# Seven small experts of a mixture-of-experts step in 64-row slots, two column tiles of plain fp32 at once

## The chip, the cores and the metric

The kernel runs on one core of one Trainium2 chip. The metric is the device time of one execution in microseconds (us): 1438.26 us, the median of 3 runs (1433.28 to 1438.53).

## What is computed

The reference is one inference step of a two-layer decoder for 512 prompt tokens and 8 samples, 520 tokens in all, of 1,024 features. Each layer has a mixer (layer 0: convolution and differential attention; layer 1: mLSTM), a layer norm, a mixture of experts, a second layer norm and a gated embedding. The part that matters here is the mixture of experts: a token chooses one of four groups and two of the group's four experts, so there are 1,040 pairs of token and expert in each layer.

```python
def hier_moe(x, w_group, w_router, w_gate, w_up, w_down):
    ...
    y = jnp.zeros_like(xt)
    for e in range(N_EXPERTS):                      # 16 experts
        hid = jax.nn.silu(xt @ w_gate[e]) * (xt @ w_up[e])   # 1024 x 512, twice
        y = y + gate[:, e:e + 1] * (hid @ w_down[e])         # 512 x 1024
    return y.reshape(b, t, d)
```

All of it is in float32. An expert's weights are 6.29 MB, so each layer reads 100.7 MB of them.

## The kernel before

`route` (L1010) works out, on VectorE, the group and the two experts of each token and each token's rank within its experts (`rank`, from 1; 0: no member). `moe` (L1049) then goes through the experts 0 to 15 in their own order, a block of 128 slots each.

For a block, `indices` (L1070) makes a one-hot matrix of ranks against slots, and from it, with small matmuls, the rows' numbers; empty slots get a number past the end. `gather` (L1086) fetches the rows by an indirect DMA on POOL. `tokens` (L1164) transposes them (8 blocks of 128) and takes each element apart into two fp32r parts, high and low. `parts` (L1175) loads a weight matrix in two loads of 1 MB and takes it apart likewise, 1,024 columns at a time: ScalarE casts (L129), VectorE subtracts (L130). `product` (L1184) and `mm3` (L133) multiply: high by high, high by low, low by high (L134 to L136), each 128 x 128 by 128 x 512. `hidden` (L1191) is silu(gate) times up, `hidden_T` (L1197) its transpose in parts, `down` (L1206) the third product, scaled by the slot's gate on ScalarE (L1223) and added to the rows of `ya` in DRAM by an indirect DMA on POOL (L1224). An expert has 24 matmuls for each of its three matrices, 72 in all. The down products of an expert come behind the next one's gate and up (only expert 13's come earlier).

Loads go through `load_w` (L138) into rings of 1 MB buffers (`wbuf`, L150): 14 buffers at first (`moe_pools`, L762), and from expert 10 on (`ESW`, L1290) the 5 buffers of two pools, as the others are wanted for what follows. Eight loads (gate and up of experts 0 and 1) are issued while the mixer ends (`moe_load`, L771). The ring's loads 8 to 13 are issued on POOL's queue, the others on SP's, in the order in which the experts need them; each waits until the buffer's last reader is done.

Behind `rank`, `moe` prepares blocks 0 and 1, then works out the gates (L1115 to L1144, `vals` as three bfloat16 parts) and, from the experts' counts, how many further blocks of 128 rows are needed (L1146 to L1159, `nbi`). Every engine reads that number (L1160) before it goes on; the further blocks (`overflow`, L1227) come behind the last expert, with weights by a register, and none are needed here. `ple_load` (L1342) queues the weights of the gated embedding behind the last expert's.

Of the kernel before, what the change touches and what calls it, by code (L numbers as in the profile page):

```python
# [8 lines left out]
F32 = mybir.dt.float32  # L9
# [3 lines left out]
I32 = mybir.dt.int32  # L13
# [9 lines left out]
T = TP + NS  # L23
# [7 lines left out]
MAXOV = (2 * T) // (CAP + 1)  # L31
# [22 lines left out]
              ("bm", 8), ("p16", 1), ("nhalf", 5), ("slots", 128), ("strict", 128), ("ids", 10), ("eidx", 16)]  # L54
# [8 lines left out]
def shape_constants():  # L63
# [29 lines left out]
    c["eidx"] = np.broadcast_to(np.arange(16, dtype=np.float32), (128, 16))  # L93
    big = np.zeros((128, CW), np.float32)
# [18 lines left out]
class K:  # L113
# [24 lines left out]
    def load_w(self, src):  # L138
        """a weight view of 8 KB per partition, into the next of the weight buffers"""
        w = self.wbuf()  # L140
        self.w_now = self.split_pools or not NW2 + NW3 < self.wturn <= GQ
# [39 lines left out]
    # work behind a product, one stage after each of the next products  # L181
# [3 lines left out]
    def behind(self, gen):  # L185
        """each stage behind what is traced by then: the weights' loads and parts and the products"""
# [17 lines left out]
    def split_w(self, w, l, h=None):  # L204
        """parts of w [128, a, c]: the low one in l [128, a * c], the high one in h or a tile of its own"""
# [5 lines left out]
    def hbuf(self):  # L211
        """a tile for a high part"""
# [4 lines left out]
    def lbuf(self):  # L217
        """a tile for two low parts, from the ring of the first weight buffers"""
# [117 lines left out]
    def to_T(self, x, n, m, xh, xl):  # L336
        """x [n tokens, 1024] -> columns of x^T, split"""
# [9 lines left out]
    def even(self):  # L347
# [4 lines left out]
        # mz: what the last rows need longest, where only parts of weights follow  # L352
        with tc.tile_pool(name="mz", bufs=1) as mz, tc.tile_pool(name="mx", bufs=1) as mx, tc.tile_pool(name="mx2", bufs=2) as mx2:
# [73 lines left out]
            # decode: rows of the cache (half page groups of 4 tokens)  # L427
# [68 lines left out]
            def attn(hp, i):  # L496
# [34 lines left out]
                # enough for the first token tile  # L531
# [3 lines left out]
            def norm_o(o, n, nh, hp, cols):  # L535
                """o [n, nh, 128]: rms norm over the last axis, scale, transpose into oT"""
# [14 lines left out]
            # convolution branch  # L551
# [41 lines left out]
            def dec_softmax():  # L593
                # decode softmax over 1024 cached keys and the new one
# [36 lines left out]
                # weight of the new token, [b, hp]  # L631
# [44 lines left out]
            # small loads, behind those of the weights  # L676
# [36 lines left out]
            def decode_tail():  # L713
                """what the samples' attention has left, and their tokens' norm"""
# [11 lines left out]
            # output projection by token tiles  # L726
# [28 lines left out]
    def mixer_pools(self):  # L755
        """what a mixer needs up to its output projection lies at the far end, where the experts' weights follow"""
# [14 lines left out]
    def moe_load(self, i, a, b):  # L771
        """the first weights of the experts, a up to b"""
# [5 lines left out]
    def norm_consts(self, p):  # L778
        """gains and offsets of the norms by feature, for both layers"""
# [13 lines left out]
    def router_consts(self):  # L793
        """router weights with the norm's gain folded in, the part of its offset, their sums negated, for both layers"""
# [21 lines left out]
    def mix_load(self, i):  # L816
        """the weights of the output projection, in rows"""
# [5 lines left out]
    def mix_split(self, own):  # L823
        """their parts: the high ones over x^T; own(k): a tile for the parts k and k + 1, where rows lie over x^T"""
# [146 lines left out]
        # router logits, of the rows before the norm, then with its mean and deviation  # L971
# [14 lines left out]
        # x1 for the experts, alpha * x1 to add their outputs to  # L986
# [13 lines left out]
    def rstd(self, tile, st, n):  # L1000
        """mean in column 0 and 1 / sqrt(var + eps) in column 3, from bn_stats"""
# [8 lines left out]
    def route(self):  # L1010
        """groups and experts of the tokens, the members of each expert and their ranks within it"""
# [7 lines left out]
        def places(l, n):  # L1019
            """how many are ahead: larger, or equal and before"""  # L1020
# [14 lines left out]
        # ranks from 1 (0: no member)  # L1035
# [13 lines left out]
    def moe(self, i):  # L1049
# [5 lines left out]
        with tc.tile_pool(name="exp", bufs=2) as p2:  # L1055
# [14 lines left out]
            def indices(rk):  # L1070
# [870 lines left out]
```

## Time and profile before

| | |
|---|---|
| median of 3 runs | 1438.26 us (1433.28 to 1438.53) |
| profiled execution | span 1429.4 us from the first to the last instruction; its own whole time is not told |
| PE (TensorE) | 1345.2 us busy, 94% of the span |
| DVE (VectorE) | 1062.8 us, 74% |
| ACT (ScalarE) | 811.3 us, 57% |
| POOL (GpSimd) | 256.8 us, 18% |
| DMA | 338.79 MB, mean 237 GB/s |
| expert stages | 345 to 661 us and 1031 to 1346 us |

How to read it: times are us from the span's start. PE's matmuls overlap one another in their pipeline, so that the work of one is seen from the start of one to the start of the next, not from its duration. The slices cut the span into 40 equal parts of 35.7 us. A window's row has for PE, PEld (weight loads of TensorE), DVE, ACT and POOL the busy us and the number of instructions, then the granted share of TensorE's clock (1.00 is 2.4 GHz, 0.50 is 1.2 GHz), the share of time in which the 16 DMA engines are busy, and GB/s. SPq is SP's sequencer, which issues DMAs; the length of such a row is the time until the issue was taken. A row of the timeline has start, length, engine, line, operation, what it writes and reads, and how many instructions were merged in it.

### The profile page before, as it was taken

Reading aid. Unit: us, or ns where it says so; the run is one execution under the profiler, and the core shown is the slowest. Engines: PE = TensorE matmul, PEld = TensorE weight load, DVE = VectorE, ACT = ScalarE, POOL = GpSimd, SP = SyncE. Lnnn points to the kernel's source line nnn. Section 1 sums busy time; section 2 is a strip of 40 time slices with the busy share of each in tenths; the row PEclk is TensorE's granted clock in tenths of the full one; section 3 lists DMA queues with packets and bytes.
Section 4 is the critical chain, followed back from the end, with each engine's and each line's share of the span. In section 5 each row is a group of like instructions: output and inputs, shape, how many; then the busy total and the mean of one; then the engine's idle time right before and its main releaser. Section 6 shows DMA issues by size and latency. Waiting matters only on the chain. (4 is left out here: it accounts for less than half of the span.)

```text
span 1429.4 us, 22095 instructions
## 1 busy us (share of the span) xinstructions
PE 1345.2 (94%) x8336; PEld 1121.1 (78%) x8336; DVE 1062.8 (74%) x1680; ACT 811.3 (57%) x1235; POOL 256.8 (18%) x262
## 2 busy tenths in 40 slices
PE   8999999995999999998989999999599999989997
PEld 7998877563888887777979988878388888867786
DVE  4679986457999998886745445775799999878672
ACT  3214554223888886777654332333378888777762
POOL 1013212324211112101130000101411111210113
PEclk9989999996999999999999999999799999999999
DMA  8458545876899969998342213483599997899821
GB/s 285 141 186 284 202 144 223 295 290 220 292 380 360 352 209 312 333 334 283 95 153 71 81 62 122 149 320 130 196 322 350 346 356 255 271 353 319 289 80 38
DMA packets 154254, 338.79 MB, mean 237 GB/s; under 512 B 17773, under 2 KB 56137, under 8 KB 150046
## 3 DMA queue, kind: packets, MB, share of 16 engines
q1 hardware_dynamic: 129438, 250.30, 49.6%
q0 software_dynamic: 24560, 86.96, 18.9%
q8 instruction: 67, 1.10, 0.3%
q14 instruction: 45, 0.37, 0.1%
q10 hardware_dynamic: 144, 0.07, 0.0%
HBM read 317.33 MB, written 36.48 MB: 248 GB/s over the span
## 5 line engine op out<-in xcount | busy, mean ns | idle before, releaser
L130 DVE TENSOR_TENSOR w<-w,sh 128x1024 fp32r<-128x1024 f32 x368 | 439.2, 1221 | 121.3 <-ACT sh L129 102.2
L129 ACT CAST sh<-w 128x1024 fp32r<-128x1024 f32 x368 | 376.0, 1050 | 247.8 <-PE acc L226 109.5
L135 PE MATMUL acc<-w,gh 128*128 128x512 f32 x512 | 204.1, 399 | 4.7 <-DVE w L130 4.4
L134 PE MATMUL acc<-sh,gh 128*128 128x512 f32 x512 | 207.2, 405 | 0.7 <-ACT sh L129 0.7
L136 PE MATMUL acc<-sh,gl 128*128 128x512 f32 x512 | 203.1, 397 | 0.8 <-DVE gl L130 0.8
L1224 POOL DMA_INDIRECT ya<-y,ix x32 | 52.2, 1631 | 386.0 <-ACT y L1223 375.9
L135 PEld LDWEIGHTS acc<-w,gh 128*128 128x128 f32 x512 | 97.3, 190 | 28.8 <-DVE w L130 8.4
L136 PEld LDWEIGHTS acc<-sh,gl 128*128 128x128 f32 x512 | 97.1, 190 | 23.9 <-DVE gl L130 1.7
L134 PEld LDWEIGHTS acc<-sh,gh 128*128 128x128 f32 x512 | 97.3, 190 | 22.8 <-ACT sh L129 1.9
L136 PE MATMUL acc<-sh,hl 128*128 128x512 f32 x256 | 102.7, 401 | 0.0
L134 PE MATMUL acc<-sh,hh 128*128 128x512 f32 x256 | 101.0, 395 | 0.9 <-ACT hh L129 0.9
L135 PE MATMUL acc<-w,hh 128*128 128x512 f32 x256 | 100.7, 394 | 0.0
L226 PE MATMUL acc<-x2h,w 128*128 128x256 f32 (+1 forms) x384 | 87.7, 291 | 0.9 <-ACT x2h L1463 0.4
L226 PE MATMUL acc<-xh,sh 128*128 128x256 f32 (+1 forms) x384 | 85.4, 301 | 2.0 <-ACT sh L129 1.2
L226 PE MATMUL acc<-xh,w 128*128 128x256 f32 (+1 forms) x384 | 81.1, 292 | 0.0
L226 PE MATMUL acc<-x3h,sh 128*128 128x256 f32 (+1 forms) x384 | 81.0, 291 | 0.0
L226 PE MATMUL acc<-xl,sh 128*128 128x256 f32 (+1 forms) x384 | 81.0, 292 | 0.0
L130 DVE TENSOR_TENSOR w<-wpair,sh 128x1024 fp32r<-128x1024 f32 x64 | 76.1, 1220 | 3.8 <-PE acc L135 2.0
L226 PE MATMUL acc<-x3l,sh 128*128 128x256 f32 (+1 forms) x384 | 78.5, 284 | 0.0
L226 PE MATMUL acc<-x3h,w 128*128 128x256 f32 (+1 forms) x384 | 78.1, 283 | 0.0
L129 ACT CAST sh<-wpair 128x1024 fp32r<-128x1024 f32 x64 | 65.6, 1051 | 14.4 <-PE acc L136 14.4
L258 PE MATMUL tps<-cst,w 128*128 128x128 f32 (+1 forms) x352 | 54.6, 287 | 13.5 <-DMA w<-xd,ix 9.3
(512 smaller groups left out, 2869.6 us busy)
## 6 DMA issues: line engine op xcount, KB each, us to landing
w<-in_w_exp_gate SPq DMA_DIRECT2D x52, 1024.0 KB
w<-in_w_exp_up SPq DMA_DIRECT2D x46, 1024.0 KB
w<-in_w_exp_down SPq DMA_DIRECT2D x46, 1024.0 KB
w<-in_w_in_even SPq DMA_DIRECT2D x12, 1024.0 KB
w<-in_w_in_odd SPq DMA_DIRECT2D x12, 1024.0 KB
wpair<-in_w_exp_up SPq DMA_DIRECT2D x10, 1024.0 KB
wpair<-in_w_exp_down SPq DMA_DIRECT2D x10, 1024.0 KB
w<-in_w_exp_down POOLq DMA_DIRECT2D x8, 1024.0 KB, 8.7
```

Of the source, the lines that this page charges most:

```text
L129: a = self.S.copy(h, src)
L130: self.sp_last = a, self.V.tensor_sub(l, src, h.bitcast(F32))
L134: self.T.matmul(ps, ah, bh, start=start, stop=False)
L135: self.T.matmul(ps, ah, bl, start=False, stop=False)
L136: self.mm3_last = self.T.matmul(ps, al, bh, start=False, stop=stop)
L226: self.mm_last = self.T.matmul(ps[t], a[:, k, :], b[:, k, t0[t]:t1[t]], start=(k == 0 and i == 0), stop=(k == nk - 1 and i == 2))
L258: self.T.transpose(out, in_, self.c("ident")[:k, :k])
L1224: G.indirect_dma_start(out=ya, out_offset=bass.IndirectOffsetOnAxis(ap=ix[:, 0:1], axis=0), in_=y, in_offset=None, bounds_check=T - 1, oob ...
```

## The change

Experts 0 and 1 stay as they are. The other 14 are taken in another order: their counts are sorted on VectorE behind the preparation of blocks 0 and 1, and the seven with the fewest rows get the slots 3, 5, ... 15 (`SMALL`), the other seven the slots 2, 4, ... 14. Ranks and gates are put in the order of the slots (`by_slot`). The weights of slots from 2 on are addressed by a register that SP reads from the sorted list (`value_load`, `dyn`), and all of them are issued on SP's queue (`now`).

A small slot holds 64 rows. The row's two halves of 512 features are gathered into partitions 0 to 63 and 64 to 127, so that four transposes give all features. Its products take the weights as they are loaded, in plain fp32, without parts: gate in columns 0 to 63 of the array and up in columns 64 to 127; for the down product the two halves of the output features. So a small expert has 16 products for gate and up and 8 for down. Its outputs are scaled and added in half rows. An expert among the seven that has more than 64 rows would get further blocks, which count from 64.

```diff
+HCAP = 64
+SMALL = tuple(range(3, NE, 2))
...
+            pc = self.tp()
+            for m in range(5):
+                TE.matmul(pc[:, :NE], self.onb, Mb[:, m, :], start=(m == 0), stop=(m == 4))
...
+            V.tensor_copy(cnt[:, 0, :], pc[:, :NE])
+            V.scalar_tensor_tensor(key, cnt[:, 0, :], 16.0, self.c("eidx"), op0=OP.mult, op1=OP.add)
+            V.tensor_tensor(lt, key[:, None, 2:].to_broadcast(ss), key[:, 2:, None].to_broadcast(ss), op=OP.is_lt)
+            V.tensor_reduce(sr[:, 2:], lt, axis=AX, op=OP.add)
+            V.tensor_tensor(sel, sr[:, None, 2:].to_broadcast(ss), self.c("rslot")[:, :, None].to_broadcast(ss), op=OP.is_equal)
+            V.tensor_tensor(lt, sel, self.c("eidx")[:, None, 2:].to_broadcast(ss), op=OP.mult)
+            V.tensor_reduce(eid[:, 2:], lt, axis=AX, op=OP.add)
+            V.tensor_copy(eii, eid[:, 2:])
+            def by_slot(out, src):
+                t = p2.tile([128, 5, ns, ns], F32, name="pick", tag="y", bufs=3)
+                V.tensor_tensor(t, src[:, :, None, 2:].to_broadcast([128, 5, ns, ns]),
+                                sel[:, None].to_broadcast([128, 5, ns, ns]), op=OP.mult)
+                V.tensor_reduce(out, t, axis=AX, op=OP.add)
+            by_slot(rs, rank)
...
+            by_slot(gs[:, :, 2:], gt)
+            self.gate_parts(vals, gs)
...
+            def half(ps, xT, src, hf):
+                ws = [self.load_w(v[hf], now=True).rearrange("p (a c) -> p a c", a=4) for v in src]
+                for a in range(4):
+                    for z in range(2):
+                        TE.matmul(ps[z * HCAP:(z + 1) * HCAP, :], xT[:, a, hf, :], ws[z][:, a, :],
+                                  start=(hf == 0 and a == 0), stop=(hf == 1 and a == 3))
...
+                    if small:
+                        for a in range(2):
+                            k = hf * 2 + a
+                            for z in range(2):
+                                self.mm3_last = TE.matmul(pd[z * HCAP:(z + 1) * HCAP, 0, :], hx[:, k, :],
+                                                          w[:, a, z * 512:(z + 1) * 512], start=(k == 0), stop=(k == 3))
...
+            def dyn(ev, n, r):
+                return [A[n][i][bass.ds(ev, 1), h * r:h * r + r, :].rearrange("o (k p) c -> p (o k) c", p=128) for h in range(2)]
...
-                wg, wu = (parts(rows(A[w][i, e], 512)) for w in ("w_exp_gate", "w_exp_up"))
+                small = e in SMALL
+                if e < 2:
+                    sg, su, sd = (rows(A[w][i, e], n) for w, n in (("w_exp_gate", 512), ("w_exp_up", 512), ("w_exp_down", 256)))
+                else:
+                    ev = nc.sync.value_load(eii[0:1, e - 2:e - 1], min_val=0, max_val=NE - 1)
+                    sg, su, sd = (dyn(ev, w, n) for w, n in (("w_exp_gate", 512), ("w_exp_up", 512), ("w_exp_down", 256)))
...
-                product(pgu[:, 0, :], gx, wg)
+                if small:
+                    half(pgu[:, 0, :], gx, (sg, su), 0)
+                else:
+                    product(pgu[:, 0, :], gx, parts(sg, e >= 2))
```

The list of further blocks is worked out as before, from counts that are raised by 64 for the seven, behind the gates.

## Rows read from the trace of the kernel before

**Rows 1.** The page's slices: granted clock and DMA share in tenths

```profile
PEclk9989999996999999999999999999799999999999
DMA  8458545876899969998342213483599997899821
```

**Rows 2.** Windows of the expert stages; columns as told above

```profile
395.00:506.00 111.00, 111.00 (x596) 91.14 (x596) 104.33 (x115) 91.45 (x103) 15.77 (x12) 1.00 1.00 357
1085.00:1186.00 101.00, 101.00 (x537) 83.13 (x536) 94.90 (x104) 83.58 (x94) 14.68 (x11) 1.00 1.01 361
506.00:569.00 63.00, 61.53 (x324) 49.95 (x322) 56.11 (x62) 48.32 (x56) 12.68 (x12) 1.00 0.79 257
...
569.00:648.00 79.00, 74.13 (x358) 58.54 (x359) 67.10 (x70) 60.78 (x68) 7.37 (x5) 1.00 0.96 339
```

**Rows 3.** Timeline of POOL: the adds of two experts that follow each other

```profile
443.43 1.58 POOL L1224 DMA_INDIRECT ya<-y,ix  x1 [11.78 <-ACT y L1223]
...
461.88 1.59 POOL L1224 DMA_INDIRECT ya<-y,ix  x1 [11.76 <-ACT y L1223]
```

**Rows 4.** Timeline of PE: two matmuls of an expert's product

```profile
427.27 0.40 PE L134 MATMUL acc<-sh,gh 128*128 128x512 f32 x1
427.51 0.39 PE L135 MATMUL acc<-w,gh 128*128 128x512 f32 x1
```

**Rows 5.** Timeline of SP: an issue that is held up, and one that isn't

```profile
463.82 3.68 SPq L147 DMA_DIRECT2D w<-in_w_exp_up  x1
...
631.68 0.37 SPq L147 DMA_DIRECT2D w<-in_w_exp_up  x1
```

**Rows 6.** Timeline of PE: one plain fp32 product over 512 columns

```profile
267.94 1.02 PE L668 MATMUL tps<-mk,eb 128*8 128x512 f32 x2
```

**Rows 7.** Timeline of PE: eight plain products in four column tiles, and their neighbours

```profile
284.33 0.39 PE L136 MATMUL acc<-xl,yl 128*128 128x512 f32 x1
284.65 1.92 PE L660 MATMUL tps<-w,a 128*32 128x512 f32 x16
286.51 0.50 PE L134 MATMUL acc<-xl,yh 128*128 128x512 f32 x1
```

**Rows 8.** Timeline of DVE behind the routing, both layers

```profile
349.92 1.22 DVE L130 TENSOR_TENSOR w<-w,sh 128x1024 fp32r<-128x1024 f32 x1
...
351.47 0.16 DVE L1158 TENSOR_REDUCE nbt<-nb 128x1 f32<-128x16 f32 x1
351.55 0.68 DVE L130 TENSOR_TENSOR gl<-tps,gh 128x512 fp32r<-128x512 f32 x1
...
352.23 0.14 DVE L1159 CAST nbi<-nbt 128x1 int32<-128x1 f32 x1
...
1037.14 0.14 DVE L1159 CAST nbi<-nbt 128x1 int32<-128x1 f32 x1
```

**Rows 9.** Timeline of POOL and SP: first loads around the routing, both layers

```profile
333.76 0.78 POOL L147 DMA_DIRECT2D wpair<-in_w_exp_gate  x1
...
353.57 6.10 SPq L147 DMA_DIRECT2D w<-in_w_exp_down  x2
...
1040.14 4.42 SPq L147 DMA_DIRECT2D w<-in_w_exp_down  x2
```

**Rows 10.** Timeline at the end of the experts: SP, POOL, and a scaling on ACT

```profile
632.10 10.96 SPq L147 DMA_DIRECT2D w<-in_w_exp_down  x4
...
659.96 1.55 POOL L1224 DMA_INDIRECT ya<-y,ix  x1 [5.10 <-ACT ph L129]
...
1344.25 1.56 POOL L1224 DMA_INDIRECT ya<-y,ix  x1 [5.09 <-ACT ph L129]
...
423.56 1.12 ACT L1223 ACTIVATE y<-acc,gs 128x1024 f32<-128x1024 f32 x1
```

**Rows 11.** Windows with TensorE waiting; columns as in rows 2

```profile
340.00:360.00 20.00, 12.16 (x69) 9.42 (x69) 16.05 (x55) 8.65 (x12) 6.48 (x8) 0.55 0.72 258
561.00:585.00 24.00, 19.69 (x101) 15.12 (x100) 17.45 (x21) 14.89 (x18) 2.73 (x3) 1.00 0.97 341
```

More of the change, by code (lines that the diff above doesn't have):

```diff
@@ L93, in shape_constants @@
     c["eidx"] = np.broadcast_to(np.arange(16, dtype=np.float32), (128, 16))
+    c["rslot"] = np.broadcast_to(np.array([SMALL.index(z) if z in SMALL else NSM + (z - 2) // 2 for z in range(2, NE)], np.float32), (128, NE - 2))
+    c["half"] = (2 * BIG + (p >= HCAP)).astype(np.float32)[:, None]
     big = np.zeros((128, CW), np.float32)
@@ L136, in mm3, with load_w @@
         self.mm3_last = self.T.matmul(ps, al, bh, start=False, stop=stop)
[L138 removed]
+    def load_w(self, src, now=False):
         w = self.wbuf()
[L141 removed]
+        self.w_now = now or self.split_pools or not NW2 + NW3 < self.wturn <= GQ
         with ExitStack() as st:
@@ L1100, in moe, with prepare @@
             blocks = []
-            def prepare(e):
-                oh, ix = indices(rank[:, :, e])
-                gather(ix, xga[e % 4])
-                blocks.append((oh, ix, xga[e % 4]))
+            def prepare(z):
+                small = z in SMALL
+                oh, ix = indices(rank[:, :, z] if z < 2 else rs[:, :, z - 2], small)
+                xg = xga[z % 4][:, 0:512] if small else xga[z % 4]
+                gather(ix, xg, small)
+                blocks.append((oh, ix, xg))
             prepare(0)
@@ L1162, in moe, with tokens @@
             self.dump(f"rank{i}", rank)
-            def tokens(xg):
+            def tokens(xg, small=False):
+                if small:
+                    xT = p2.tile([128, 4, 2, HCAP], F32, name="xT", tag="gh")
+                    ps = self.tp().rearrange("p (a b) -> p a b", a=4)
+                    for j in range(4):
+                        self.tr_block(ps[:, j, :], xg[:, j * 128:(j + 1) * 128], 128)
+                    S.copy(xT.rearrange("p a z b -> p a (z b)"), ps)
+                    return xT
                 gh = p2.tile([128, 8, 128], F32R, name="gh")
@@ L1195, in hidden, with hidden_T @@
                 return hid
-            def hidden_T(hid):
+            def hidden_T(hid, small=False):
+                if small:
+                    hx = p2.tile([128, 4, HCAP], F32, name="hx", tag="hh", bufs=1)
+                    ps = self.tp()[:, 0:4 * HCAP].rearrange("p (a b) -> p a b", a=4)
+                    for j in range(4):
+                        self.tr_block(ps[:, j, :], hid[:, j * 128:(j + 1) * 128], HCAP)
+                    self.hid_last = S.copy(hx, ps)
+                    return hx
                 hh = p2.tile([128, 4, 128], F32R, name="hh", bufs=1)
@@ L1204, in hidden_T, with down @@
                 return hh, hl
-            def down(ix, gate, hx, src, end=False):
+            def down(ix, gate, hx, src, now, small, end=False):
                 pd = self.acc()
-                ws = [self.load_w(v) for v in src] if end else None
+                ws = [self.load_w(v, now) for v in src] if end else None
                 if end:
@@ L1222, in down @@
                 y = p2.tile([128, D], F32, name="y", bufs=3)
+                if small:
+                    S.mul(y[:, 0:512], pd[:, 0, :], gate)
+                    G.indirect_dma_start(out=rows2(ya), out_offset=bass.IndirectOffsetOnAxis(ap=ix[:, 0:1], axis=0),
+                                         in_=y[:, 0:512], in_offset=None, bounds_check=2 * T - 1, oob_is_err=False, compute_op=OP.add)
+                    return
                 S.mul(y.rearrange("p (a b) -> p a b", a=2), pd, gate)
@@ L1274, in overflow @@
                         gate = gates(oh, lambda m: vo[:, m, :])
[L1275 to L1276 removed]
                         gx, pgu = tokens(xo), self.acc()
[L1278 to L1280 removed]
+                        product(pgu[:, 0, :], gx, parts(dyn(ev, "w_exp_gate", 512), True))
+                        product(pgu[:, 1, :], gx, parts(dyn(ev, "w_exp_up", 512), True))
+                        down(ix, gate, hidden_T(hidden(pgu)), dyn(ev, "w_exp_down", 256), True, False)
             rows = lambda w, n: [w[h * n:h * n + n, :].rearrange("(k p) c -> p k c", p=128) for h in range(2)]
@@ L1313, in moe @@
                 gate = gates(oh, lambda m, e=e: vals[:, m, e, :])
-                product(pgu[:, 1, :], gx, wu)
-                hid = hidden(pgu)
+                if small:
+                    half(pgu[:, 0, :], gx, (sg, su), 1)
+                else:
+                    product(pgu[:, 1, :], gx, parts(su, e >= 2))
+                hid = hidden(pgu, small)
                 if last and e != NE - 2:
-                    down(*last[:2], hx, last[3])
-                last = ix, gate, hid, rows(A["w_exp_down"][i, e], 256)
+                    down(*last[:2], hx, *last[3])
+                last = ix, gate, (hid, small), (sd, e >= 2, small)
                 gx = gx_next
             with tc.high_priority():
-                hx = hidden_T(last[2])
-            down(*last[:2], hx, last[3], end=True)
+                hx = hidden_T(*last[2])
+            down(*last[:2], hx, *last[3], end=True)
             with tc.issue_after(self.mm3_last.ins):
```

87 lines of the change are left out of this document (53 added, 34 removed).

## The prediction

> **What bounds the kernel now.** I read the slices of the page first, then the windows of the two expert stages (340 to 660 us and 1030 to 1345 us), then the queues in them. The slices show TensorE at its upper level, 2.4 GHz, almost everywhere, and the DMA engines nearly full in the two stages that hold the experts and only there [rows 1]. The windows say it in numbers: in 395 to 506 and in 1085 to 1186 us TensorE is busy for all of the stretch and the DMA share is 1.00 and 1.01 at 357 and 361 GB/s [rows 2]. So two resources are full at once there. The adds of one expert's rows into `ya` follow each other at 18.45 us [rows 3], and that is TensorE's pace: 72 matmuls of 0.23 us from start to start [rows 4] are 16.6 us, and 1.9 us are left for transposes, slots and gates. That the DMA side has no room either is seen on SP: an issue takes 0.37 us when its queue has room, and 3.68 us at 463.8 us, where SP waits for no buffer but for the queue itself [rows 5]. In 506 to 569 us the share falls to 0.79: the ring of weight buffers is changed at expert 10, and its first buffers come free late. In 569 to 648 us it is 0.96 at 339 GB/s, with TensorE busy 74.1 of 79 us [rows 2].
>
> What an expert costs the DMA engines: six loads of 1.049 MB are 6.29 MB, and its rows, 65 on the mean (1,040 pairs of token and expert over 16), go through a gather and an add of 4 KB each, 0.53 MB. 6.82 MB at 359 GB/s are 19.0 us, a little more than the 18.45 us in which TensorE now uses them up. The experts run on what was fetched ahead.
>
> **The change, part by part.**
>
> TensorE. A plain fp32 product over 512 columns shows as two records 0.43 us apart (1.02 less one record's 0.59), so 0.86 us [rows 6]. Whether two products in different columns of the array run at once is shown by the cached values' product, eight plain products of 32 columns in four column tiles: sixteen records take 1.86 us up to the start of the next matmul, where one after the other they would take 8 x 0.86 = 6.9 us [rows 7]. So a set of tiles costs what one product does. A small expert has 8 pairs for gate and up and 4 for down: 12 x 0.86 = 10.3 us. Entering and leaving the tiles costs 0.09 us ahead (0.32 in place of 0.23) and 0.14 us behind (1.86 less 4 x 0.43) [rows 4, 7], three times per small expert: 0.7 us. With the unchanged 1.9 us (four row transposes fewer, not credited) a small expert takes 12.9 us in place of 18.45, and seven in two layers free 78 us of TensorE. The bounds of this price are 0.86 us per pair (tiles at once) and 1.72 us (in turn); I take the first, since the row with column tiles is much nearer than any with a full array.
>
> A rule that speaks against this stands in the Trainium skill, TensorEngine Tiling (Array Packing), Key Properties: a change of the tiling mode drains TensorE. The rows agree that there is a price, 0.23 us a visit; with a whole record's 0.59 us instead, the small expert would come to 14.0 us, and the sum below would not change.
>
> ScalarE and VectorE lose the parts of seven experts, 12 casts and 12 subtractions each. Neither is the bound in rows 2, so this is worth nothing.
>
> The loads. The bytes stay: the same 96 loads per layer, the same rows gathered and added (half rows of 2 KB, twice as many). Since the DMA engines are full, 5.6 us less of TensorE per small expert turns into waiting for weights. What they can still give is their idle time: in 506 to 569 us 0.21 x 63 = 13 us per layer. That hole goes, as TensorE, starved by then, uses expert 9's weights as they land, and expert 10's loads follow at once.
>
> What the change costs there is the start. Before, the four gate and up loads of expert 2 went out on POOL from 333.8 us on, ahead of the routing's end, and SP's first load (down of expert 1) at 353.6 us, 1.3 us after the count of further blocks, `nbi` [rows 8, 9]. Now the loads of all slots from 2 wait, on SP, for the sorted numbers, and ahead of them in SP's queue stands the read of `nbi`, which itself comes behind the new work on VectorE. That is: some five operations on 196 elements, taken at 0.35 us between the rows over 16 and 512 elements (0.16 and 0.68 us), and five smaller ones at 0.16 us, together 2.5 us; and twice a multiplication over 980 elements and its sum, no such sum being in the trace. I take 1.22 us each, the row over 1,024 elements, for all four [rows 8]; half or double that would move the start by 2.4 us down or 4.9 us up. Sum 7.4 us, all of it on the path to `nbi`. Queued behind the waiting SP are down of expert 1 and all later loads; the rows for slots 2 and 3 wait for the sorted ranks too, but are needed 25 us later. First load in layer 0: 352.4 + 7.4 + 1.3 = 361 us; in layer 1: 1037.3 + 7.4 + 2.9 = 1047.6 us [rows 8, 9]. The reads themselves (14 per layer on SP) have no row; SP spends 6 x 0.37 of each 19 us on issuing, so anything up to some microseconds each is covered by the loads in flight, and would cost the excess if the cover were gone.
>
> From there 86 loads are left (84, and down of expert 1): 48 up to the change of rings, 50.3 MB and 4.3 MB of rows at 359 GB/s, 152 us; 38 after it, 39.8 and 3.2 MB at 339 GB/s, 127 us. With 2 us for the first to land the last weights are there at 361 + 281 = 642 us and 1047.6 + 281 = 1328.6 us.
>
> The end. Before, the last of the four last loads was out by 643.1 us and the last add is issued at 659.96 us, since two whole experts' worth of down products, with their parts, stood behind it [rows 10]. Now slot 15 is small: two pairs (1.7 us) after its last load, a scaling of half of 1.12 us [rows 10], the issue: 3 us. Last add at 645 in place of 660.0, and at 1331.6 in place of 1344.3 us. Against that, the 1.5 MB for the gated embedding still come behind the last weights, and now no down products cover them: 4.2 us at 359 GB/s against these 3 us, and then the gate's first 2 MB; I take 3 us lost per layer. 12.0 + 9.7 = 21.7 us.
>
> **Sum.** The profiled execution has a span of 1429.4 us, and 8.9 us less than the median 1438.26 of the runs. I take the gain off the median: 1438.3 - 21.7 = 1416.6, **1416 us**. TensorE's own sum, from 350 us: 9 x 18.45 + 7 x 12.9 = 256 us to 606 us, so it isn't the bound.
>
> **The rivals.**
>
> *Column tiles in turn (slower).* At 1.72 us per pair a small expert takes 23.2 us, and seven cost 33 us of TensorE per layer; some 6 us per layer of waiting before (1.5 and 4.9 us in the last two windows) would be used up [rows 2], so 27 us per layer: about 1490 us. It decides once a pair costs more than 1.4 us (a small expert over 19 us). Against it are rows 7. Chance 0.07.
>
> *The late start eats it all.* With 339 GB/s throughout, 97.6 MB take 288 us; 9 us more per layer, 1435 us. For it: the long ring's 359 GB/s was reached with only full experts, and twice as many small packets may cost more; against it: the rows' bytes are a twelfth. Chance 0.2.
>
> *Transfers faster than I think, TensorE the bound.* Last add at about 609 us, 50 us per layer less: near 1340 us. Against it: the share of 1.00 and SP's blocked issues [rows 2, 5]. Chance 0.05; in between, 380 GB/s would give 257 us per layer in place of 279 and 1372 us.
>
> *A starved TensorE falls to 1.2 GHz.* In 340 to 360 us it was busy for 12.2 of 20 us, and the granted clock was 0.55; in 561 to 585 us for 19.7 of 24, at 1.00 [rows 11]. Waits in a small slot (12.9 of 19 us busy) lie between. If each small slot of the starved part (five of seven) ran at half clock, 25.8 + 18.45 = 44 us per two experts would exceed the 38 us of the loads: 30 us per layer, 1476 us. The Trainium skill's TensorE: Matmul & The Clock Gate, Loop structure matters more than you think, warns of just such DMA waits between matmuls. Chance 0.05.
>
> *The change doesn't do what it says:* an expert among the seven with over 64 rows goes through a further block of 128, its loads exposed: about 40 us. The reference's own routing of its inputs gives seven smallest of 44, 45, 52, 58, 59, 63, 64 rows in layer 0 and 49 to 61 in layer 1, so none, but 64 is the edge. Chance 0.03.
>
> **How the numbers follow.** My case has 0.6: weights as the bound, 1416 us, and 1378 to 1435 us between 375 and 339 GB/s. It lies almost wholly on the faster side. About 0.5% (7 us) is what a measurement of this kernel can tell from no change. Faster by more than that (below 1431 us): 0.57 of my case, 0.04 of the second, 0.05 of the third: 0.66. Same: 0.18, from the second and my case's edge. Slower: 0.16, the first, the last two, and a dearer start. The range reaches from 1378 us to 1444 us.
>
> **What would show it.** In the profile after: `half` records in groups 0.43 us apart, two at once, 0.86 us a pair; in 370 to 640 us a DMA share near 1.0 without the hole at 506 to 569 us, and 340 to 360 GB/s; TensorE busy for some 80% there, waiting for `w`; SP's first dynamic load near 361 us; the last add near 645 us. It would be wrong if the adds come at 13 us for small slots throughout (transfers not the bound), if pairs take 1.7 us, if the granted clock drops in the expert stage, or if the DMA share falls below 0.9 with loads not yet issued, the new wait on SP.

## The result and the profile after

The changed kernel takes 1400.87 us, median of 4 runs (1397.97 to 1403.28); the kernel before, run beside it, 1435.77 us (1432.82 to 1438.53). The ratio is 0.975, with a 95% interval of 0.9721 to 0.9778: 34.9 us less. The forecast was 1416 us within 1378 to 1444, so the sign and the range held, and the gain was 13.2 us more than the 21.7 us of the sum. The profiled executions have spans of 1429.4 and 1401.5 us, 27.9 us apart: the one before is a quick one of its runs and the one after a slow one, so lengths of stages are compared below, not points of time.

The page's busy times and slices of the kernel after, beside [rows 1]:

```profile
PE 1293.0 (92%) x7944; PEld 987.0 (70%) x7944; DVE 857.8 (61%) x1500; ACT 628.7 (45%) x1053; POOL 250.8 (18%) x242
...
PEclk9989999997799999999999999999879999999999
DMA  7548644893899999999352223384379999999821
```

VectorE lost 205 us and ScalarE 183 us, as the parts of fourteen experts are gone; TensorE lost 52 us of busy time. Where the two stages begin, the granted clock (in tenths, two slices each) now reads 77 in place of 69, and 87 in place of 79.

The windows of the first stage, cut as in [rows 2], columns as there:

```profile
395.00:506.00 111.00, 111.00 (x592) 72.37 (x591) 72.88 (x86) 63.79 (x76) 23.47 (x14) 1.00 1.00 356
506.00:569.00 63.00, 58.40 (x303) 34.62 (x304) 32.28 (x41) 30.77 (x39) 11.63 (x8) 0.97 0.95 333
569.00:648.00 79.00, 67.74 (x293) 38.29 (x291) 32.25 (x36) 30.73 (x41) 6.65 (x5) 0.96 1.00 349
```

In 506 to 569 us the DMA share rose from 0.79 to 0.95 and the rate from 257 to 333 GB/s: the hole is all but closed. TensorE now waits more in the last two windows: it is busy for 58.4 of 63 and 67.7 of 79 us, before for 61.5 and 74.1.

From the first gather of a stage to its last add, the kernel before takes 315.6 and 313.9 us. The rows of POOL after give 647.60 less 348.83 = 298.8, and 1316.65 less 1015.87 = 300.8 us:

```profile
348.83 1.11 POOL L1101 DMA_INDIRECT w<-xd,ix  x1 [4.18 <-DVE sgx L1163]
396.63 1.63 POOL L1312 DMA_INDIRECT ya<-y,ix  x1 [11.13 <-ACT y L1311]
...
446.78 1.59 POOL L1308 DMA_INDIRECT ya<-y,ix  x1 [9.67 <-ACT y L1307]
461.49 1.59 POOL L1312 DMA_INDIRECT ya<-y,ix  x1 [8.47 <-ACT y L1311]
478.81 1.58 POOL L1308 DMA_INDIRECT ya<-y,ix  x1 [9.62 <-ACT y L1307]
...
545.54 1.58 POOL L1308 DMA_INDIRECT ya<-y,ix  x1 [15.47 <-ACT y L1307]
...
583.13 1.58 POOL L1308 DMA_INDIRECT ya<-y,ix  x1 [15.51 <-ACT y L1307]
...
647.60 1.55 POOL L1308 DMA_INDIRECT ya<-y,ix  x1 [5.23 <-DVE w L138]
```

So the two stages are 16.8 and 13.1 us shorter, 29.9 us together; outside them the profiled execution after is 2.0 us longer than the one before. The first add comes 47.8 us behind the first gather, where before it was 43.6 (387.96 less 344.38): the stage begins 4.2 us slower. Adds of a small and a full slot together take 32.0 us (446.78 to 478.81), before 2 x 18.45 = 36.9. That is still close to TensorE's own pace (31.2 us in a run below), on weights that were fetched ahead; from 545.54 to 583.13 such a pair takes 37.6 us, near the 38 us that two experts' transfers need. So the transfers set the pace only in the later part of the stage.

### The profile page after: what moved, and what is told of

The parts are those of the page before. It is cut to its first block, busy times and chain, and to the rows that moved or that the text cites. A ratio compares the mean times of both kernels' runs of the same rounds, so it can differ in the third digit from the quotient of the medians.

```text
span 1401.5 us, 21016 instructions
## 1 busy us (share of the span) xinstructions
PE 1293.0 (92%) x7944; PEld 987.0 (70%) x7944; DVE 857.8 (61%) x1500; ACT 628.7 (45%) x1053; POOL 250.8 (18%) x242
## 5 line engine op out<-in xcount | busy, mean ns | idle before, releaser
L138 DVE TENSOR_TENSOR w<-w,sh 128x1024 fp32r<-128x1024 f32 x224 | 267.6, 1221 | 124.4 <-ACT sh L137 104.4
L137 ACT CAST sh<-w 128x1024 fp32r<-128x1024 f32 x224 | 228.0, 1048 | 197.9 <-PE acc L234 108.1
L143 PE MATMUL acc<-w,gh 128*128 128x512 f32 x288 | 119.6, 415 | 7.3 <-DVE w L138 7.3
L142 PE MATMUL acc<-sh,gh 128*128 128x512 f32 x288 | 119.0, 413 | 3.4 <-ACT sh L137 3.4
L144 PE MATMUL acc<-sh,gl 128*128 128x512 f32 x288 | 117.6, 408 | 0.0
L1251 PE MATMUL acc<-w,xT 128*64 128x512 f32 x432 | 109.8, 597 | 3.3 <-DMA w<-in_w_exp_up 3.3
L1101 POOL DMA_INDIRECT w<-xd,ix x32 | 47.6, 1488 | 140.2 <-DVE gs L1111 84.0
L234 PEld LDWEIGHTS acc<-x2h,w 128*128 128x128 f32 x384 | 64.5, 189 | 2.5 <-issue 1.3
L234 PEld LDWEIGHTS acc<-xh,sh 128*128 128x128 f32 x384 | 63.6, 198 | 3.6 <-ACT sh L137 1.7
L234 PEld LDWEIGHTS acc<-xh,w 128*128 128x128 f32 x384 | 63.0, 198 | 0.7 <-DVE w L138 0.6
```

The source lines that it names most:

```text
L137: a = self.S.copy(h, src)
L138: self.sp_last = a, self.V.tensor_sub(l, src, h.bitcast(F32))
L142: self.T.matmul(ps, ah, bh, start=start, stop=False)
L143: self.T.matmul(ps, ah, bl, start=False, stop=False)
L144: self.mm3_last = self.T.matmul(ps, al, bh, start=False, stop=stop)
L234: self.mm_last = self.T.matmul(ps[t], a[:, k, :], b[:, k, t0[t]:t1[t]], start=(k == 0 and i == 0), stop=(k == nk - 1 and i == 2))
```

## The experiments

The theory when they began: before, TensorE set the pace; after, it is the weights' transfers, and what TensorE saves beyond them turns into waiting. The rivals: TensorE still sets it; the sort, the late start or the end costs much of the gain; part of the gain isn't from the small slots at all.

**Half the products, all the bytes.**

```diff
-                for a in range(4):
+                for a in (0, 3):
```

> The changed kernel, with half of the gate and up products of the small experts left out (two of the four pairs per weight tile are issued; their part of the contraction is missing); all loads, gathers and adds stay. TensorE loses 4 pairs of 0.86 us = 3.4 us per small expert, 24 us per layer, 48 us in all. Theory (the weights' transfers bound the expert stage of the changed kernel): 1388 to 1401 us, and what comes off is only the end of each layer, where the last slot's products stand behind the last load (3.4 us per layer). Rival (TensorE is still the bound and the gain goes with its time): 1401 - 48 = 1353 us.

1398.05 us (1394.92 to 1403.47), ratio 0.9743 (0.97 to 0.9787). Of 48 us of TensorE's work, 2.8 us come through, less than can be told from nothing. TensorE waits more, the transfers run on:

```profile
506.00:569.00 63.00, 53.80 (x247) 35.70 (x245) 34.11 (x38) 31.54 (x37) 8.66 (x6) 0.92 0.98 341
```

So less work on TensorE alone doesn't make the changed kernel faster.

**Half the bytes, all the products.**

```diff
-                ws = [self.load_w(v[hf], now=True).rearrange("p (a c) -> p a c", a=4) for v in src]
+                ws = [self.load_w(v[hf][:, 0:2, :], now=True).rearrange("p (a c) -> p a c", a=4) for v in src]
...
-                        TE.matmul(ps[z * HCAP:(z + 1) * HCAP, :], xT[:, a, hf, :], ws[z][:, a, :],
+                        TE.matmul(ps[z * HCAP:(z + 1) * HCAP, :], xT[:, a, hf, :], ws[z][:, a % 2, :],
```

> The changed kernel, with each gate and up load of a small expert cut to half its bytes (0.52 MB in place of 1.05 MB; the half that is loaded is used twice, so the other half of these weights is left out); the products keep their number and size. 28 x 0.52 = 14.7 MB less per layer, 40.9 us at 359 GB/s; TensorE's own sum, 256 us from the first expert's start, sets in after 25 to 36 us of these. Theory (transfers bound): 1325 to 1355 us. Rival (TensorE bound): unchanged, 1396 to 1403 us. If in between (1360 to 1390), the two resources are near balance and the late start or the end takes the rest.

1376.55 us (1373.6 to 1377.89), ratio 0.9594 (0.956 to 0.9627): 24 us less, between the two ranges, in what I had called near balance. In 395 to 506 us, where TensorE is full in the changed kernel too, the DMA share is now 0.88 in place of 1.00; in 506 to 569 us TensorE is busy for 61.2 us in place of 58.4, and the DMA share is still 0.94:

```profile
395.00:506.00 111.00, 111.00 (x622) 70.77 (x620) 72.75 (x86) 64.94 (x78) 22.86 (x14) 1.00 0.88 305
506.00:569.00 63.00, 61.18 (x308) 37.26 (x309) 32.38 (x40) 28.65 (x37) 10.92 (x7) 1.00 0.94 329
569.00:636.00 67.00, 58.98 (x275) 34.69 (x272) 30.19 (x35) 32.08 (x47) 7.80 (x5) 0.95 0.91 307
...
440.37 1.58 POOL L1308 DMA_INDIRECT ya<-y,ix  x1 [8.84 <-ACT y L1307]
455.09 1.59 POOL L1312 DMA_INDIRECT ya<-y,ix  x1 [8.49 <-ACT y L1311]
471.57 1.58 POOL L1308 DMA_INDIRECT ya<-y,ix  x1 [8.79 <-ACT y L1307]
```

Here TensorE's own pace is seen: 440.37 to 471.57 is 31.2 us for a small and a full slot. My 12.9 + 18.45 were 31.35.

**Both cuts at once.** The two edits above together.

> The changed kernel with both cuts of the first runs at once: each gate and up load of a small expert with half its bytes, and half of the products on it (half of these experts' contraction is left out). Alone, half the products gave 3 us and half the bytes 24 us of a possible 82 (40.9 us per layer). Theory (transfers and TensorE are near balance in the changed kernel, TensorE some 12 us per layer below, so that with the bytes halved TensorE sets the pace): the products now count too, up to 24 us per layer, 1330 to 1350 us. Rival (what is left is the start and the end of the stage, and neither resource): 1368 to 1378 us.

1357.18 us (1354.8 to 1359.11), ratio 0.9451 (0.9419 to 0.9483). The cut in products that gave 2.8 us with all the bytes gives 19.4 us with half of them. That is 7 us short of the theory's range and 11 us beyond the rival's; what takes the rest is not shown. So the changed kernel stands where the two resources nearly meet: transfers first, TensorE with its waits some 12 us per layer behind.

**Gate and up in the same column tile.**

```diff
-                        TE.matmul(ps[z * HCAP:(z + 1) * HCAP, :], xT[:, a, hf, :], ws[z][:, a, :],
+                        TE.matmul(ps[0:HCAP, z, :], xT[:, a, hf, :], ws[z][:, a, :],
...
-                    V.tensor_tensor(hid, pgu[HCAP:2 * HCAP, 0, :], hid, op=OP.mult)
+                    V.tensor_tensor(hid, pgu[0:HCAP, 1, :], hid, op=OP.mult)
```

> The changed kernel, with gate and up of a small expert both in the first 64 columns of the array, into two banks, so that no pair of them can run at once (down keeps its two column tiles). If a product alone takes 0.86 us, a small expert gets 8 x 0.86 = 6.9 us dearer, 19.8 us in place of 12.9, and TensorE's sum per layer, 9 x 18.45 + 7 x 19.8 = 305 us, passes the 281 us of the loads: 1430 to 1460 us. If the tiles do not run at once in the changed kernel either, or TensorE has more room than I think: 1398 to 1406 us.

1454.84 us (1449.4 to 1462.95), ratio 1.0139 (1.0083 to 1.0195): slower than before the change. The adds around a small slot stand 21.6 us apart in place of 14.7, 6.9 us more, as worked out:

```profile
449.34 1.58 POOL L1308 DMA_INDIRECT ya<-y,ix  x1 [8.97 <-ACT y L1307]
470.91 1.59 POOL L1312 DMA_INDIRECT ya<-y,ix  x1 [11.91 <-ACT y L1311]
```

The whole gain hangs on the two tiles running at once; the relief of VectorE and ScalarE, which this run keeps, alone brings nothing.

**Sort and registers without small slots.**

```diff
-SMALL = tuple(range(3, NE, 2))
+SMALL = ()
...
-    c["rslot"] = np.broadcast_to(np.array([SMALL.index(z) if z in SMALL else NSM + (z - 2) // 2 for z in range(2, NE)], np.float32), (128, NE - 2))
+    c["rslot"] = np.broadcast_to(np.array([z - 2 for z in range(2, NE)], np.float32), (128, NE - 2))
```

> The other part of the change alone: sort, register loads on SP for slots 2 to 15 and ranks and gates by slot as in the changed kernel, but no slot is small, every expert runs in 128 rows as before. TensorE's sum is that of the kernel before, 16 x 18.45 = 295 us and some 20 us up to the first add, 315 us per layer. Theory (the sort and the later loads are covered, since TensorE is the bound with full slots, and the loads that the kernel before sends on POOL after the change of rings now go out on SP as well, which shortens the hole there): 1423 to 1437 us. Rival (the later start costs what I had forecast, 9 to 10 us per layer): 1445 to 1457 us.

1443.29 us (1436.92 to 1448.15), ratio 1.0045 (1.0027 to 1.0064): 6.5 us slower than before, between the two ranges, so the sort is neither covered nor as dear as forecast. Against this run the small slots bring 42 us. The hole is still there, 0.74 at 249 GB/s, though all loads are on SP:

```profile
506.00:569.00 63.00, 63.00 (x348) 51.87 (x347) 59.27 (x67) 50.58 (x57) 8.90 (x7) 1.00 0.74 249
```

**The kernel before with the later loads on SP.** In the kernel before, eight loads per layer behind the change of rings are issued on POOL; the change's `now` moved them to SP, which my prediction had missed.

```diff
-        self.w_now = self.split_pools or not NW2 + NW3 < self.wturn <= GQ
+        self.w_now = self.on_sp or self.split_pools or not NW2 + NW3 < self.wturn <= GQ
...
-                    self.wpools, self.wturn = self.ring(RS), 0
+                    self.wpools, self.wturn, self.on_sp = self.ring(RS), 0, True
```

> The kernel before with one thing of the change: from expert 10 on, where the ring of weight buffers is changed, all weight loads are issued on SP; in the kernel before, eight of them per layer (540 to 558 us in layer 0) are issued on POOL. Theory (these eight are what makes the hole at 506 to 569 us, as SP's queue stands still meanwhile): its waits go, some 7 us per layer, 1420 to 1430 us. Rival (the hole comes of the buffers of the short ring, whichever queue loads them): 1432 to 1440 us.

1431.15 us (1425.8 to 1434.21), ratio 0.996 (0.9942 to 0.9979): 5.6 us less, just outside the theory's range on the small side. The hole itself stays (0.81 at 272 GB/s), so it isn't made by the queue, which adds a few us to it; that leaves the short ring and the pace at which buffers come back. Taken with the run above, sort, registers and the later loads of slot 2 cost 6.5 + 5.6 = 12 us where TensorE is the bound. Ten of these lie between the first gather and the first add, which is 47.5 and 49.0 us in the run above and 43.5 and 43.2 us here, before any weight of slot 2 is used: there the sort's work on VectorE is paid.

**The order of the experts written into the program.** No sort and no registers; ranks and gate values are read in place.

```diff
-                oh, ix = indices(rank[:, :, z] if z < 2 else rs[:, :, z - 2], small)
+                oh, ix = indices(rank[:, :, EXP[i][z]], small)
...
-                    ev = nc.sync.value_load(eii[0:1, e - 2:e - 1], min_val=0, max_val=NE - 1)
-                    sg, su, sd = (dyn(ev, w, n) for w, n in (("w_exp_gate", 512), ("w_exp_up", 512), ("w_exp_down", 256)))
+                sg, su, sd = (rows(A[w][i, EXP[i][e]], n) for w, n in (("w_exp_gate", 512), ("w_exp_up", 512), ("w_exp_down", 256)))
```

> The changed kernel without the sort on the chip and without registers: the order of the experts that these inputs give is written into the program, ranks and gate values are read in place, and the loads of slot 2 go out early on POOL again, as in the kernel before, SP's without a wait for the routing. Small slots and column tiles stay. Theory (the transfers bound the stage, so that each microsecond of an earlier start comes through): four loads of 1.05 MB, 11.7 us at 359 GB/s, are ahead of the routing's end in each layer: 1376 to 1392 us. Rival (the start is covered by what experts 0 and 1 have to do, the weights come early enough): 1397 to 1403 us.

1398.07 us (1396.82 to 1406.22), ratio 0.976 (0.9715 to 0.9805): no difference. But this version had also got the eight loads on POOL back, and with them a worse hole. SP's timeline there:

```profile
518.72 23.57 SPq L159 DMA_DIRECT2D w<-in_w_exp_gate  x2
542.39 0.47 SPq L159 DMA_DIRECT2D w<-in_w_exp_up  x1
```

SP's two issues are held for 23.6 us while the loads come by POOL. So once more, with only slot 2's loads on POOL (`now` for slots from 3):

> The static order of the experts again, with only slot 2's loads early on POOL and all others on SP, so that the eight loads on POOL after the change of rings, which the static version had got back, are on SP as in the changed kernel. Theory (an earlier start of the transfers comes through; the first static version gave it back at the change of rings, where its adds are 24.6 and 27.7 us apart): 1378 to 1391 us. Rival (the ring of buffers is full early in any case, TensorE sets the pace up to slot 6, so the start is worth little): 1393 to 1402 us.

1387.34 us (1383.05 to 1388.37), ratio 0.966 (0.9632 to 0.9687): 13.5 us less than the changed kernel. By the range this was the theory's case, the early start. The rows point elsewhere:

```profile
343.28 1.10 POOL L1105 DMA_INDIRECT w<-xd,ix  x1 [3.45 <-DVE cnt L1139]
385.26 2.25 POOL L1288 DMA_INDIRECT ya<-y,ix  x1 [9.58 <-ACT y L1287]
...
1004.94 1.11 POOL L1105 DMA_INDIRECT w<-xd,ix  x1 [2.07 <-DVE sge L1144]
1047.23 2.24 POOL L1288 DMA_INDIRECT ya<-y,ix  x1 [9.54 <-ACT y L1287]
```

Gather to first add is 42.0 and 42.3 us, in the changed kernel 47.8 and 49.0 (1064.90 less 1015.87): 12.5 of the 13.5 us are won before the first expert's rows are out, before any expert from slot 2 is used. From first to last add the stages are only 1.2 and 1.7 us shorter. What stands there in the changed kernel is the sort's own work on VectorE, ahead of expert 0's parts; TensorE's timeline after:

```profile
363.89 0.40 PE L1091 MATMUL tps<-idr,oh 128*128 128x1 bf16 x10
365.44 0.40 PE L1091 MATMUL tps<-idr,oh 128*128 128x1 bf16 x10 [1.15 <-DVE oh L1086]
367.89 0.80 PE L143 MATMUL acc<-w,gh 128*128 128x512 f32 x1 [2.05 <-DVE w L138]
368.49 0.63 PE L144 MATMUL acc<-sh,gl 128*128 128x512 f32 x1
368.91 0.63 PE L142 MATMUL acc<-sh,gh 128*128 128x512 f32 x1
```

and VectorE's in those us:

```profile
363.42 1.17 DVE L1153 TENSOR_TENSOR pick<-gt,sel 128x980 f32<-128x980 f32 x1
...
365.30 1.17 DVE L1155 TENSOR_REDUCE gts<-pick 128x70 f32<-128x980 f32 x1
...
366.62 1.22 DVE L138 TENSOR_TENSOR w<-w,sh 128x1024 fp32r<-128x1024 f32 x1
```

TensorE waits 1.15 and 2.05 us for VectorE, and its matmuls then follow at 0.42 us in place of 0.23. Two windows of the changed kernel, then one of the static kernel:

```profile
356.00:390.00 34.00, 30.80 (x160) 24.68 (x159) 31.08 (x58) 20.74 (x24) 6.12 (x5) 0.85 0.96 345
366.00:372.80 6.80, 4.91 (x12) 3.85 (x13) 5.97 (x12) 1.05 (x1) 1.78 (x2) 0.51 0.99 368
```

```profile
356.00:390.00 34.00, 34.00 (x206) 27.80 (x205) 31.52 (x38) 28.08 (x31) 7.32 (x4) 1.00 0.90 303
```

From 367.89 to 372.75 us twelve matmuls run at half clock, 4.9 us in place of 2.8; with the waits that makes 5.3 us more, near the 5.8 us by which the first add of this layer comes later than in the static kernel. The rest of the 0.85 is the half clock at which the stage begins (0.50 up to 358.7 us). The static kernel begins so too, but ahead of this window, since its gather is 5.6 us earlier; it has no second drop.

**Three fixed experts, so that slot 2 can be loaded early with the sort in place.** Experts 0 to 2 keep slots 0 to 2, the other 13 are sorted, six slots are small; slots 5, 7, ... 15 first, then 3, 5, 7, 9, 11 and 15.

```diff
-SMALL = tuple(range(3, NE, 2))
+SMALL = tuple(range(5, NE, 2))
+NF = 3
...
-                if e < 2:
+                if e < NF:
```

> The changed kernel with three experts in fixed slots in place of two, so that slot 2 has a static address and its four gate and up loads go out early on POOL again; the sort and the registers stay, over the other 13 experts, and six of them are small (slots 5, 7, ... 15; the six with the fewest rows have 44 to 64 and 49 to 57). One small slot less is 5.5 us more of TensorE per layer, in the stage where it has room. Theory (what the static order gained, 1387 us, is the early start of slot 2's transfers, and neither the sort nor the register loads cost anything beside it): 1383 to 1394 us. Rival (the static order gained because sort and registers were gone): 1397 to 1404 us.

1405.01 us (1403.3 to 1409.41), ratio 0.9773 (0.9756 to 0.979). A us beyond the rival's range. Before I took it for the rival's case I tried whether the five full slots at the start had eaten the lead:

> Three fixed experts and six small ones again, with the same work on every engine as in the run that took 1405 us, but with the small slots at 3, 5, 7, 9, 11 and 15 in place of 5, 7, ... 15. In that run the DMA share in 356 to 390 us was 0.79, where the changed kernel has 0.96: five full slots in a row gave buffers back at TensorE's 18.4 us, and the early loads' lead went while SP waited for buffers. Theory (the lead of slot 2's loads is kept if the small slots begin at once; sort and registers cost nothing beside it): 1385 to 1396 us. Rival (the sort and the registers are what the static order saved, or six small slots are too few): 1400 to 1408 us.

1398.91 us (1396.74 to 1404.41), ratio 0.9747 (0.9707 to 0.9787), between the ranges and no different from the changed kernel. The place of the small slots is worth some 6 us by the medians, though the two runs' ranges touch; but with slot 2's loads early the first add still comes 47.1 us behind the first gather in layer 0 (45.6 in layer 1, so 4 of the 12.5 us are back):

```profile
341.21 1.10 POOL L1102 DMA_INDIRECT w<-xd,ix  x1 [3.45 <-DVE cnt L1142]
...
388.34 2.25 POOL L1313 DMA_INDIRECT ya<-y,ix  x1 [9.34 <-ACT y L1312]
```

So early loads with the sort still there don't bring back what the static order won. One small slot less costs TensorE 5.5 us per layer here, so that a small worth of the loads could be hidden behind it; the share of the sort and that of the early loads in the 13.5 us were not separated.

**Down of slot 14 earlier.**

```diff
-                    if e == NE - 2:
+                    if e >= NE - 2:
                         down(*last[:2], hx, *last[3])
...
-                if last and e != NE - 2:
+                if last and e < NE - 2:
```

> The changed kernel, with the down product of slot 14 (its loads, parts and matmuls) put ahead of the second half of slot 15's gate and up, in place of behind it. In the changed kernel the last add comes 10.7 us after the last weights, since down of slot 14 with its parts stands behind slot 15's products. Theory: 3 to 7 us less per layer, 1388 to 1396 us. Rival (the loads for the gated embedding, not this chain, set when the next stage can go on): 1398 to 1404 us.

1401.2 us (1391.35 to 1403.54), ratio 0.9737 (0.9706 to 0.9768): nothing, the rival's case. The last add did come earlier, 643.40 us, 295.7 us behind the first gather (347.7) in place of 298.8, and it was given back: the next stage's first store `x3d` comes 34.2 us behind the last add in place of 30.5. Rows of this run, then of the changed kernel:

```profile
634.74 8.06 SPq L1470 DMA_DIRECT2D w<-in_w_ple_gate  x2
643.40 1.55 POOL L1308 DMA_INDIRECT ya<-y,ix  x1 [9.31 <-ACT y L1307]
677.57 0.85 POOL L1595 DMA_DIRECT2D x3d<-st  x1 [4.38 <-ACT st L1589]
```

```profile
637.14 6.51 SPq L1470 DMA_DIRECT2D w<-in_w_ple_gate  x2
...
678.06 0.85 POOL L1595 DMA_DIRECT2D x3d<-st  x1 [4.38 <-ACT st L1589]
```

**The gated embedding's projection ahead of the last products.** The edit above, and `ple_load`'s first three loads within slot 14, `ple_parts` and all of `ple_proj` ahead of the second half of slot 15:

```diff
+                if e == NE - 2:
+                    self.ple_load(i, 0)
+                if e == NE - 1:
+                    with tc.issue_after(self.mm3_last.ins):
+                        self.ple_parts(p2)
+                    self.ple_proj(range(8))
```

> The changed kernel with down of slot 14 early, as in the run that showed no gain, and with the gated embedding's first 1.5 MB (its projection and its rows) loaded within slot 14 in place of behind the last weights, its parts and all of its projection's products put ahead of the second half of slot 15. Theory (behind the last add the next stage waits for this projection, some 11 us of products from 649 to 660 us, whatever the add's time is; in the stage itself TensorE has room for them): 4 to 9 us less per layer, 1383 to 1393 us. Rival (the next stage waits for the gate's own weights or for the rows that are read back from DRAM): 1396 to 1403 us.

1436.65 us (1431.34 to 1441.57), ratio 1.0002 (0.9982 to 1.0021): 36 us worse, outside both ranges. The work was moved in front of slot 15's products and delayed them, and nothing came back behind the add, though the projection was done by then:

```profile
648.83 6.37 SPq L1475 DMA_DIRECT2D w<-in_w_ple_gate  x2
655.95 1.82 POOL L1308 DMA_INDIRECT ya<-y,ix  x1 [21.52 <-ACT y L1307]
690.87 0.85 POOL L1599 DMA_DIRECT2D x3d<-st  x1 [5.18 <-ACT st L1593]
```

34.9 us from the last add to the first store. So neither the last add nor the projection alone sets the next stage's pace. What stays nearly the same is the distance from the second load of the gate's weights (the end of the merged row) to the first store: 34.4 us in the changed kernel, 34.8 with the early down, 35.7 here, and 35.0 before the change (656.76 to 691.75). That points to the gate's weights, whose loads wait for buffers; no run moved them alone, so it isn't shown.

Of the kernels that sort on the chip none was measurably faster than the changed one. The static order is, by 13.5 us, but it holds for these inputs alone.

## Why the prediction was right, and which steps failed

*Column tiles.* As forecast. Four pairs of gate and up:

```profile
412.66 0.39 PE L144 MATMUL acc<-sh,hl 128*128 128x512 f32 x1
412.99 3.65 PE L1251 MATMUL acc<-w,xT 128*64 128x512 f32 x16
416.57 1.09 PE L266 MATMUL tps<-cst,w 128*128 128x128 f32 x8
```

3.58 us from start to start, 4 x 0.86 and 0.14 behind; ahead 0.33 in place of 0.23. The rule on drains (the Trainium skill, TensorEngine Tiling (Array Packing), Key Properties) agrees with these 0.24 us a visit.

*Both resources full, transfers the bound.* Right by the two cuts, for the stage as a whole; up to some 510 us the changed kernel still runs at TensorE's pace on what was fetched ahead, as I had it for the kernel before. But I put TensorE's sum at 606 us, 36 us below the loads' 642, and called it not the bound. With the bytes halved the last add comes at 630.1 us, 286.1 us behind the first gather and only 12.7 us below the changed kernel (10.1 in layer 1). I expected TensorE busy for some 80% of the stage; the three windows after have 237 of 253 us, 94%. The pace of the slots was right; what I left out of TensorE's chain are the slow start (below) and waits that stay even with half the bytes: in that run it is busy 61.2 of the 63 us from 506 and, as its window from 569 to 636 us shows, 59.0 of 67 us.

*The hole.* That it closes is right, and the reason, buffers that come back sooner, fits: the run without small slots still has the hole, and so has the run with gate and up in turn (0.69 at 231 GB/s in 506 to 569 us), which has small slots but not their pace. That eight loads per layer also change their queue was in the diff (`now`) and in no term of my sum; in the kernel before it is worth 5.6 us in all.

*The start* failed. I had SP's loads from slot 2 wait for the read of `nbi` and forecast the first at 361 us, 16.6 us behind the gather, all of it paid by the end of the loads. The rows after:

```profile
354.60 0.16 DVE L1148 CAST eii<-eid 128x14 int32<-128x14 f32 x1
...
362.27 0.15 DVE L1207 CAST nbi<-nbt 128x1 int32<-128x1 f32 x1
```

```profile
355.93 1.04 SPq L155 DMA_DIRECT2D wpair<-in_w_exp_gate  x2
```

SP goes on 1.2 us behind the sorted numbers, 7.1 us behind the gather, and doesn't stop for `nbi`. The price of VectorE's new work was right (1.17 us in place of 1.22, 0.35 as taken), its place was wrong: it isn't paid on SP's queue but in front of expert 0's parts, where it makes TensorE wait and then run at 1.2 GHz. The first add is later by 4.2 us in layer 0 and 7.1 in layer 1 (49.0 less 41.9, 1072.25 less 1030.36 before), where I had 7.4 us in each, on SP's first load. I never asked who else stood behind that work on VectorE's queue.

*The rate and the end of the loads.* 359 and 339 GB/s were forecast, 356 and 333 to 349 came. The start being earlier, the last of the weights is issued at 630.92 us, 282 us behind the gather.

*The end* failed. I had the last add 3 us behind the last load. Before it stand slot 14's down products with their parts, which I had left in "two whole experts' worth" of the kernel before and let vanish:

```profile
632.68 0.50 PE L142 MATMUL acc<-sh,hh 128*128 128x512 f32 x1
...
639.58 3.65 PE L1295 MATMUL acc<-w,hx 128*64 128x512 f32 x16 [0.23 <-ACT hx L1271]
```

They take 632.68 to 639.2 us, and slot 15's down products wait for the hidden values behind them, not for weights; the add comes 16.7 us behind the last issue. Earlier loads and a later end cancel: 300.6 and 301.2 us from gather to last add were forecast, 298.8 and 300.8 came. That the lengths agree so well is luck. And the early down showed that this add doesn't set the time.

*The sum.* Of the 15 us by which I was low, 2.5 are the base (1438.3 against 1435.8 when measured again) and 2.2 the stages. 6 us are the term for the gated embedding's loads, 3 us lost per layer: from last add to first store it is 30.5 us after against 31.8 before in layer 0, and 30.2 us in both in layer 1, so nothing is lost. The remaining 4 us or so have no cause that the rows show; they are within the scatter of the runs.

*The rivals.* Tiles in turn: they aren't, and the run that puts gate and up in turn costs 54 us. The late start didn't eat the gain. TensorE isn't the bound, but it is nearer to being one than I had it; the 1340 us of that rival were too low, since even with half the bytes the time is 1376.6 us. No further block ran: the adds are 32, of 18 full and 14 small slots in the two layers. A starved TensorE at 1.2 GHz came in part: 0.97 and 0.96 in the last two windows, which is 3.8 + 6.3 = 10 us at half clock in a stage with some 16 us of waits, so it cost little, and in the 4.9 us of matmuls behind the sort's waits at the start of layer 0, where no wait covers it and it cost 2.1 us. What the Trainium skill says of waits between matmuls (TensorE: Matmul & The Clock Gate, Loop structure matters more than you think) agrees with the rows in kind: the clock fell behind waits, and more so with half the products (0.92). The waits at the start were for VectorE, not for a DMA, and only 1.15 and 2.05 us long.

## What to carry to other kernels

When two resources are full at once, price both chains to their ends, with what stands ahead of the first product and behind the last: here the loser of the two was only 12 us behind, and that is all that halving the other's bytes gave. New work on an engine is paid by whoever is queued behind it there, so look for the next consumer on that engine's queue and not only for the reader of the result. An add or a store that ends a stage is worth moving only if the next stage waits for it.

## What the runs showed of the hardware

Two plain fp32 products in 64-column tiles side by side take the 0.86 us of one; eight such pairs per slot put in turn made the slot 6.9 us dearer. A wait of 2.05 us, with one of 1.15 us ahead of it, was followed by matmuls at 0.42 us in place of 0.23; from 366.0 to 372.8 us the granted clock was 0.51. And loads that were shared between SP's queue and POOL's while the buffers were short held SP for 23.6 us; with only slot 2's loads left on POOL the same kernel is 10.7 us faster.
